# Five load buffers in place of three for the FFN's weights and the first FFN's modulation

## The chip, the cores and the metric

The kernel runs on one core of a Trainium2 chip. The metric is the device time of one execution in microseconds (us); lower is better. The kernel before took 2551.44 us, the median of three runs (2548.18 to 2554.93).

## What is computed

Two layers of a decoder on 256 tokens of width 2048 in float32. A conditioning vector c gives each layer six rows of 2048 numbers, the modulation. Each layer mixes tokens and then applies a SwiGLU FFN of width 5632, each behind an RMS norm that is scaled and shifted by the modulation, and each added to x through a gate from the modulation.

```python
c_act = silu(c)
for l in range(2):
    mod = c_act @ w_mod[l] + b_mod[l]                      # 2048 x 12288 weights
    shift1, scale1, gate1, shift2, scale2, gate2 = split(mod, 6)
    h = rms_norm(x, norm1_gain[l]) * (1 + scale1) + shift1
    x = x + gate1 * hybrid_token_mixer(h, ...)             # w_in, three mixers, w_out
    h = rms_norm(x, norm2_gain[l]) * (1 + scale2) + shift2
    x = x + gate2 * ((silu(h @ w_gate[l]) * (h @ w_up[l])) @ w_down[l])
return rms_norm(x, final_norm_gain)
```

All weights are read from device memory in each execution, about 600 MB with everything.

## The kernel before

**A job.** The large products run as a stream of jobs. A job is one 128 x 1024 block of weights, 512 KB. `load` brings it into a tile `raw` (line 321, issued on SP's queue). ACT rounds it into a tile `wh` (line 328), DVE takes the rest, `wl = raw - wh` (line 329), and `products` multiplies it on TensorE (PE, line 356): three terms (high by high, high by low, low by high), two column halves and two blocks of 128 tokens make 12 matmuls of 512 columns. An FFN has 264 such jobs: columns of w_gate and w_up in pairs of 512-column chunks, and the rows of w_down in two groups, after chunks 0 to 5 and 6 to 10. At the end of a pair of chunks DVE multiplies silu(gate) by up (line 1136, tile `s`), PE transposes it (line 401) and ACT and DVE split it into the left operands for w_down.

**The modulation.** It runs in the background: after each job `tick` adds a rate and, when the sum passes one, takes the next step of `mod_segment`. A step loads 512 KB of w_mod into a tile `mraw` (line 218, SP's queue too) and multiplies and adds it on DVE (line 221, SCALAR_TENSOR_TENSOR, below STT). In the first FFN the rate is 0.4 steps a job (0.6 in its first pair of chunks), in the second 0.25. The first step of an FFN waits for the norm: POOL copies one number of the norm's last high part `hm` into the `mraw` tile ahead of its load (line 216, `hold`). Finished segments are summed over partitions with a few small PE instructions (`fin`).

**Buffers.** Tiles come from pools, and a tile of a tag goes round the pool's buffers:

```python
    rawp = ctx.enter_context(tc.tile_pool(name="rawp", bufs=3))
    modp = ctx.enter_context(tc.tile_pool(name="modp", bufs=3))
    wsp = ctx.enter_context(tc.tile_pool(name="wsp", bufs=3))
```

So the load of job n waits until `wl` of job n-3 has been computed from the same buffer. `wh` and `wl` have three buffers each, and ACT's split of job n waits for PE's matmuls of job n-3. Each FFN opens a pool of its own, `ffn_0` and `ffn_1`, in memory that the mixers have left.

**The order.** The program is written in order of dataflow, and a scheduler then sets the order of each engine's instructions; the engines and SP's queue keep to it. The FFN begins while the output projection ends: the norm ahead of the FFN (lines 439 to 449: scale on DVE, transpose on PE, scale and shift on ACT, tile `s`, and a split into `hm` on ACT and DVE) runs for the two token blocks, and PE fills the gaps with the FFN's first jobs. In the second FFN a load of the final gain, tile `fg`, 1 MB, also stands on SP's queue there (line 1126).

Of the kernel before, what the change touches and what calls it, by code (L numbers as in the profile page):

```python
# [19 lines left out]
P = 128  # L20
# [4 lines left out]
DEPTH = 2  # L25
# [78 lines left out]
def trunk(ctx: ExitStack, tc, x, cT, pos, small, consts, b_mod, w_mod, w_in, w_gk, w_out,  # L104
# [4 lines left out]
    rawp = ctx.enter_context(tc.tile_pool(name="rawp", bufs=3))  # L109
    modp = ctx.enter_context(tc.tile_pool(name="modp", bufs=3))  # L110
# [16 lines left out]
    def tl(pool, shape, tag, dt=F32, bufs=None):  # L127
        return pool.tile(shape, dt, tag=tag, name=nm(tag), bufs=bufs)
# [18 lines left out]
        return ap.to_broadcast(shape)  # L147


    ct = tl(kp, [P, N_FULL], "consts")  # L150
    SY.dma_start(ct, consts[:, :N_FULL])
    n_mask = CONSTS.shape[1] - N_FULL
# [27 lines left out]
    for name, turn in (("sin", 0.0), ("cos", 0.25)):  # L180
        n = tl(kp, [P, NB, 8], "turns" + name)
# [17 lines left out]
    def mod_segment(l, part, k0, nk):  # L199

        width = nk * P
        early = l == 0 and part in (SHIFT1, SCALE1)
        rows = (512 if early else 1024) // width
        st = {}

        def step(i):
            c0 = part * D + k0 * P
            if i == 0:
                st["acc"] = scr[1]() if early else tl(accp, [P, 1024], "acc")
                G.memset(st["acc"][:, :width], 0.0)  # L210
                SY.dma_start(st["acc"][0:1, :width], b_mod[l:l + 1, c0:c0 + width])
            acc = st["acc"][:, :width]
            n = min(rows, KD - i)
            raw = scr[1]() if early else tl(modp, [P, 1024], "mraw")
            if hold:
                G.tensor_copy(raw[:, 0:1], hold.pop())
            raw = raw[:, :n * width].rearrange("p (a n) -> p a n", a=n)
            SY.dma_start(raw, w_mod[l, i * P:(i + n) * P, c0:c0 + width]
                         .rearrange("(a p) n -> p a n", p=P))
            for a in range(n):  # L220
                V.scalar_tensor_tensor(acc, raw[:, a], c_act[:, i + a:i + a + 1], acc,  # L221
                                       ALU.mult, ALU.add)
            if i + n == KD:
                fins.append([FIN_LAG, lambda: finish(acc)])

        def finish(acc):
            if part in (GATE1, GATE2):
                g = tl(gatep, [P, 1024], "gate")
                for j in range(width // 512):
                    src = acc[:, j * 512:(j + 1) * 512]  # L230
                    t = tl(modp, [P, 2, 512], "mraw", F32R)
                    A.activation(t[:, 0], src, AF.Copy)
                    V.tensor_tensor(t[:, 1], src, t[:, 0].bitcast(F32), ALU.subtract)
                    ps = tl(psf, [P, 512], "fin")
                    for i in range(2):
                        TE.matmul(ps, ones_r, t[:, i], start=i == 0, stop=i == 1)  # L236
                    A.activation(g[:, j * 512:(j + 1) * 512], ps, AF.Copy)
                    gate_row[l, part, k0 // 4 + j] = g[:, j * 512:(j + 1) * 512]
                return
            t = tl(smp, [P, nk], f"mod{part}_{k0}_{nk}")  # L240
            sums = tl(smp, [P, nk], f"sums{nk}")
            for j in range(0, nk, 4):
                ps = tl(psf, [P, 512], "fin")
                n = min(4, nk - j)
                for i in range(n):
                    TE.transpose(ps[:, i * P:(i + 1) * P],  # L246
                                 acc[:, (j + i) * P:(j + i + 1) * P], ident)
                V.tensor_reduce(sums[:, j:j + n],
                                ps[:, :n * P].rearrange("p (a b) -> p a b", a=n), AX.X, ALU.add)
            if part in (SHIFT1, SHIFT2):  # L250
                V.tensor_copy(t, sums)
            else:
                o = (0 if part == SCALE1 else KD) + k0
                V.scalar_tensor_tensor(t, sums, 1.0, gains[:, l, o:o + nk],  # L254
                                       ALU.add, ALU.mult)
            for j in range(nk):
                mod_col[l, part, k0 + j] = t[:, j:j + 1]

        return [((l, part), lambda i=i: step(i)) for i in range(0, KD, rows)]


# [29 lines left out]
    def stream(groups, ks, lhs, whole=(), lead=(), tail=()):  # L291
# [19 lines left out]
        def load(job, n, place):  # L311
            segs, _, offs, runs, _, _, k = job
            width = sum(s[2] for s in segs)
            if k in whole:
                which[1] += 1
                pool, tag = ((rawp, "raw"), (wsp, "wh"), (wsp, "wl"))[which[1] % 3]
                raw = tl(pool, [P, 1024], tag)
            else:
                raw = tl(rawp, [P, 1024], "raw")
            for w, c, m, o in runs:  # L320
                SY.dma_start(raw[:, o:o + m], w[k * P:(k + 1) * P, c:c + m])
            cuts = [(raw[:, o:o + s[2]], s[2]) for s, o in zip(segs, offs)]
            if k in whole:
                return [(r, None) for r, _ in cuts]
            if place is None:
                wh = tl(wsp, [P, 1024], "wh", F32R)
                wl = tl(wsp, [P, 1024], "wl", F32R)
                A.activation(wh[:, :width], raw[:, :width], AF.Copy)  # L328
                V.tensor_tensor(wl[:, :width], raw[:, :width], wh[:, :width].bitcast(F32),  # L329
                                ALU.subtract)  # L330
                return [(wh[:, o:o + s[2]], wl[:, o:o + s[2]]) for s, o in zip(segs, offs)]
            res = []
            for r, m in cuts:
                wh, wl = place()[:, :m], place()[:, :m]
                A.activation(wh, r, AF.Copy)
                V.tensor_tensor(wl, r, wh.bitcast(F32), ALU.subtract)  # L336
                res.append((wh, wl))
            return res
# [36 lines left out]
    def ahead(wsp_n, hm_n):  # L375
        return (None,) * wsp_n + (at_hm,) * hm_n
# [79 lines left out]
    scr = [None, None]  # L456
# [490 lines left out]
    def layer(l):  # L947
        wi, wo = w_in[l], w_out[l]
        load_small(l)
        blocks, at = [], 0  # L950
# [91 lines left out]
        for bi, ks in enumerate(blocks):  # L1042
# [8 lines left out]
            if l == 0 and first:  # L1051
                for o in range(0, n_mask, 512):
                    n = min(512, n_mask - o)
# [64 lines left out]
        with ExitStack() as st:  # L1118
            pl = st.enter_context(tc.tile_pool(name=f"ffn_{l}", bufs=1, reuse_waits="tile"))
            scr[0] = lambda: tl(pl, [P, 512], "s", bufs=8)  # L1120

            closed.discard((l, GATE2))
            if l == DEPTH - 1:
# [26 lines left out]
            for chunks in (range(0, 6), range(6, 11)):  # L1150
# [15 lines left out]
                for half in range(2):  # L1166
                    gemm([(wd, half * 1024, 512), (wd, half * 1024 + 512, 512)],
                         [c * 4 + i for c in chunks for i in range(4)], lhs_a,
                         lambda blk, j, ps, half=half, final=final: add_gated(
                             l, GATE2, blk, half * 2 + j, ps, final),  # L1170
                         tail=ahead(*TAIL_FFN) if half and final else ())

    for l in range(DEPTH):
        layer(l)
# [41 lines left out]
```

## Time and profile before

| | |
|---|---|
| median of three runs | 2551.44 us (2548.18 to 2554.93) |
| the profiled execution | 2549.07 us |
| its span, first to last instruction | 2547.1 us |
| first FFN | about 547 to 1326 us of the span |
| second FFN | about 1785 to 2530 us |
| mean granted TensorE clock | 0.99 |
| read from device memory | 597 MB, 235 GB/s over the span |

The page gives the busy time of each engine. A row of instructions reads: line, engine, operation, tile written <- tiles read, shape, count, busy time, mean duration, and in brackets or behind a bar the idle time before it and what ended it. PEld is TensorE's loading of weights, which overlaps its matmuls. A row of windows gives for a stretch of the span the busy time of PE, PEld, DVE, ACT and POOL (with instruction counts), the granted TensorE clock as a share of full speed, the busy share of the DMA engines and GB/s. A row of waits gives who waited for whom, us in total, times, and the longest. SPq rows are DMA issues on SP's queue; their length is the issue's, not the transfer's. For several merged issues (x3) it runs from the first to the last.

### The profile page before, as it was taken

To read this page: it belongs to the slowest core of one execution; us is meant where nothing else is said; L and a number is where in the kernel's file an instruction comes from. 1 tells how busy PE (TensorE), PEld (TensorE's weight loads), DVE (VectorE), ACT (ScalarE), POOL (GpSimd) and SP (SyncE) were. 2 spreads that over 40 slices of the span, in tenths; PEclk is the share of its full clock that TensorE was granted. 3 is DMA by queue.
4 is the path that set the end of the run, shared out by engine and by line. 5 is a ranking of instruction groups with operands and counts; after the bars stand their busy time and mean duration, and the time that the engine had idled before them with its cause. 6 is when DMAs were issued, how large, how long until landed. Compare 5 with 4: busy or idle time off the path is not lost. (4 is left out here: it accounts for less than half of the span.)

```text
span 2547.1 us, 30770 instructions
## 1 busy us (share of the span) xinstructions
PE 2422.7 (95%) x11164; PEld 1881.8 (74%) x11164; DVE 1715.0 (67%) x2171; ACT 1052.3 (41%) x1546; POOL 57.3 (2%) x117
## 2 busy tenths in 40 slices
PE   4999999999999999999989999989999999999998
PEld 2555886458778777888768778867777888888876
DVE  7767977667777677657677775897666455554554
ACT  2103444044444333444344554555534443344443
POOL 1000000000000000000000000000000000000000
PEclk9999999999999999999999999999999999999999
DMA  9996568849888778778778841765778655666654
GB/s 345 374 335 209 181 193 274 291 172 316 280 274 304 262 263 281 267 219 286 233 245 284 287 117 55 257 221 174 253 258 272 189 187 187 190 187 194 187 178 157
DMA packets 190031, 600.76 MB, mean 236 GB/s; under 512 B 21628, under 2 KB 26268, under 8 KB 189496
## 3 DMA queue, kind: packets, MB, share of 16 engines
q1 hardware_dynamic: 189880, 598.81, 71.2%
q8 instruction: 87, 1.43, 0.2%
q14 instruction: 64, 0.52, 0.1%
HBM read 596.63 MB, written 2.10 MB: 235 GB/s over the span
## 5 line engine op out<-in xcount | busy, mean ns | idle before, releaser
L356 PE MATMUL acc<-wh,hm 128*128 128x512 f32 (+3 forms) x4872 | 1333.4, 388 | 17.3 <-ACT acc L414 5.1
L328 ACT ACTIVATE wh<-raw 128x1024 fp32r<-128x1024 f32 (+3 forms) x669 | 685.1, 1026 | 1012.2 <-PE acc L356 575.5
L329 DVE TENSOR_TENSOR wl<-raw,wh 128x1024 fp32r<-128x1024 f32 (+3 forms) x669 | 785.7, 1179 | 464.2 <-ACT wh L328 461.0
L356 PEld LDWEIGHTS acc<-wh,hm 128*128 128x128 f32 x4872 | 890.7, 189 | 212.4 <-issue 20.3
L356 PE MATMUL acc<-wl,hm 128*128 128x512 f32 (+3 forms) x2484 | 793.3, 394 | 6.2 <-DVE wl L329 4.8
L356 PEld LDWEIGHTS acc<-wl,hm 128*128 128x128 f32 x2484 | 458.3, 189 | 116.2 <-issue 18.7
L221 DVE SCALAR_TENSOR_TENSOR acc<-mraw,c_act,acc 128x1024 f32<-128x1024 f32 x320 | 410.1, 1282 | 156.8 <-DMA mraw<-in_w_mod 154.1
L356 PE MATMUL acc<-wh,ahl 128*128 128x512 f32 x560 | 157.8, 396 | 0.0
L356 PEld LDWEIGHTS acc<-wh,ahl 128*128 128x128 f32 x560 | 105.6, 189 | 24.5
L221 DVE SCALAR_TENSOR_TENSOR g<-g,c_act,g 128x512 f32<-128x512 f32 x128 | 88.7, 746 | 11.5 <-DMA g<-in_w_mod 11.5
L356 PE MATMUL acc<-wl,ahl 128*128 128x512 f32 x280 | 90.7, 397 | 3.0 <-DVE wl L329 3.0
L356 PE MATMUL acc<-wh,b 128*128 128x512 f32 (+2 forms) x184 | 72.8, 535 | 2.2 <-ACT b L445 2.1
L356 PE MATMUL acc<-raw,b 128*128 128x512 f32 (+2 forms) x176 | 66.6, 517 | 0.0
L356 PE MATMUL acc<-wl,b 128*128 128x512 f32 (+2 forms) x176 | 66.1, 512 | 0.2 <-DVE g L967 0.2
L356 PEld LDWEIGHTS acc<-wl,ahl 128*128 128x128 f32 x280 | 52.6, 189 | 17.2 <-DVE wl L329 5.2
L356 PEld LDWEIGHTS acc<-wh,b 128*128 128x128 f32 x184 | 34.8, 194 | 31.7 <-issue 23.6
L927 DVE TENSOR_TENSOR acc<-acc,gate 128x512 f32<-128x512 f32 x64 | 42.8, 692 | 20.0 <-PE acc L356 20.0
L445 ACT ACTIVATE b<-mm,mod,mod 128x128 f32<-128x128 f32 x24 | 9.2, 458 | 108.9 <-DVE mod L254 91.3
L356 PEld LDWEIGHTS acc<-wl,b 128*128 128x128 f32 x176 | 32.6, 190 | 26.7 <-issue 21.5
L356 PEld LDWEIGHTS acc<-raw,b 128*128 128x128 f32 x176 | 32.7, 190 | 26.1 <-issue 21.8
L210 POOL MEMSET acc<- 128x1024 f32 x20 | 19.0, 954 | 1019.4 <-PE fin L246 709.7
L929 DVE TENSOR_TENSOR xs<-xs,acc 128x512 f32<-128x512 f32 x64 | 41.6, 678 | 0.1
(312 smaller groups left out, 1639.7 us busy)
## 6 DMA issues: line engine op xcount, KB each, us to landing
mraw<-in_w_mod SPq DMA_DIRECT2D x320, 512.0 KB
raw<-in_w_down SPq DMA_DIRECT2D x176, 512.0 KB
raw<-in_w_gate SPq DMA_DIRECT2D x160, 512.0 KB
raw<-in_w_up SPq DMA_DIRECT2D x160, 512.0 KB
raw<-in_w_in SPq DMA_DIRECT2D x72, 512.0 KB
g<-in_w_mod SPq DMA_DIRECT2D x128, 256.0 KB
raw<-in_w_out SPq DMA_DIRECT2D x43, 512.0 KB
raw<-in_w_in SPq DMA_DIRECT2D x32, 264.0 KB
```

The source lines that it names most:

```text
L210: G.memset(st["acc"][:, :width], 0.0)
L221: V.scalar_tensor_tensor(acc, raw[:, a], c_act[:, i + a:i + a + 1], acc, ALU.mult, ALU.add)
L328: A.activation(wh[:, :width], raw[:, :width], AF.Copy)
L329: V.tensor_tensor(wl[:, :width], raw[:, :width], wh[:, :width].bitcast(F32), ALU.subtract)
L356: TE.matmul(ps[blk, j][:, :segs[j][2]], xa, parts[j][part], start=i == 0 and n == 0, stop=last and n == len(terms) - 1)
L445: A.activation(h32[:, i], ps[:, i * P:(i + 1) * P], AF.Identity, scale=mod_col[l, 3 * sub + 1, at + i], bias=mod_col[l, 3 * sub, at + i])
L927: V.tensor_tensor(ps, ps, need(gate_row, (l, part, j)), ALU.mult)
L929: V.tensor_tensor(x_j, x_j, ps, ALU.add)
```

## The change

During an FFN the `raw` tiles take turns over five buffers, three of the pool `rawp` and two with the tag `raw2` in the FFN's own pool. In the first FFN the `mraw` tiles do the same, with `mraw2`. The turn is counted in the program's order, it goes on from where the stage before left it, and the counts are cleared at the end of each FFN. In the `finish` of a gate the tile `mraw` still comes from the three. All line numbers below the new function move by 9 (321 is now 330, 218 is 227).

```diff
+    room, turns = {}, {}
+
+    def in_turn(pool, tag, n):
+        more, m = room.get(tag, (None, 0))
+        at = turns[tag] = (turns.get(tag, -1) + 1) % (n + m)
+        return tl(pool, [P, 1024], tag) if at < n else tl(more, [P, 1024], tag + "2", bufs=m)
...
-            raw = scr[1]() if early else tl(modp, [P, 1024], "mraw")
+            raw = scr[1]() if early else in_turn(modp, "mraw", 3)
...
-                raw = tl(rawp, [P, 1024], "raw")
+                raw = in_turn(rawp, "raw", 3)
...
         with ExitStack() as st:
             pl = st.enter_context(tc.tile_pool(name=f"ffn_{l}", bufs=1, reuse_waits="tile"))
             scr[0] = lambda: tl(pl, [P, 512], "s", bufs=8)
+            room["raw"] = pl, 2
+            if l < DEPTH - 1:
+                room["mraw"] = pl, 2
...
+            room.clear()
+            turns.clear()
```

The scheduler gives another order. Three places follow, as rows of one engine: line, operation, tile written <- tensor or tile read, shape. The number that ends a tile's name tells the job: in the first FFN 4021 is job 0, 4043 job 1, 4068 job 2, 4086 job 3, 4107 job 4, 4128 job 5; in the second 14080, 14102, 14120, 14138, 14156, 14174.

SP's queue at the start of the first FFN, before:

```order
L321 DMA raw_1031_4021<-in_w_gate 128x1024
L211 DMA acc_1041_4061<-in_b_mod 1x1024
L321 DMA raw_1038_4043<-in_w_gate 128x1024
L321 DMA raw_1043_4068<-in_w_gate 128x1024
L211 DMA acc_1181_4763<-in_b_mod 1x1024
L321 DMA raw_1046_4086<-in_w_gate 128x1024
L321 DMA raw_1050_4107<-in_w_gate 128x1024
L321 DMA raw_1054_4128<-in_w_gate 128x1024
L218 DMA mraw_1049_4104<-in_w_mod 128x1024
L218 DMA mraw_1042_4064<-in_w_mod 128x1024
```

and now:

```order
L330 DMA raw_1031_4021<-in_w_gate 128x1024
L220 DMA acc_1041_4061<-in_b_mod 1x1024
L227 DMA mraw_1053_4125<-in_w_mod 128x1024
L227 DMA mraw_1060_4164<-in_w_mod 128x1024
L330 DMA raw_1046_4086<-in_w_gate 128x1024
L227 DMA mraw_1067_4203<-in_w_mod 128x1024
L220 DMA acc_1181_4763<-in_b_mod 1x1024
L330 DMA raw_1050_4107<-in_w_gate 128x1024
L330 DMA raw_1054_4128<-in_w_gate 128x1024
L330 DMA raw2_1038_4043<-in_w_gate 128x1024
L227 DMA mraw2_1042_4064<-in_w_mod 128x1024
L330 DMA raw2_1043_4068<-in_w_gate 128x1024
```

Jobs 1 and 2 have the added buffers and their loads now stand behind those of jobs 3 to 5, and job 2's behind a load into `mraw2`, which is the one that POOL's copy holds for the norm (the tile numbered 4064, as before). On ACT the same place reads now

```order
L457 ACTIVATE hm_1022_3985<-s_1021_3984 128x512
L454 ACTIVATE s_1026_4000<-mm_1030_4005,mod3_8_8_949_3713,mod4_8_8_998_3894 128x128 x3
L457 ACTIVATE hm_1027_4001<-s_1026_4000 128x512
L337 ACTIVATE wh_1039_4045<-raw2_1038_4043 128x1024
L337 ACTIVATE wh_1044_4070<-raw2_1043_4068 128x1024
L337 ACTIVATE wh_1047_4088<-raw_1046_4086 128x1024
```

where `hm_1027_4001` is the norm's last high part. Before, `wh` of jobs 1 and 2 stood ahead of the norm's first `s`, and `wh` of job 3 just ahead of that last `hm`.

SP's queue at the start of the second FFN, before:

```order
L321 DMA raw_3128_14080<-in_w_gate 128x1024
L321 DMA raw_3135_14102<-in_w_gate 128x1024
L321 DMA raw_3138_14120<-in_w_gate 128x1024
L321 DMA raw_3141_14138<-in_w_gate 128x1024
L321 DMA raw_3144_14156<-in_w_gate 128x1024
L321 DMA raw_3147_14174<-in_w_gate 128x1024
L218 DMA mraw_3214_14535<-in_w_mod 128x1024
L1126 DMA fg_3127_14078<-in_final_gain 128x2048
```

and now:

```order
L330 DMA raw_3128_14080<-in_w_gate 128x1024
L330 DMA raw_3141_14138<-in_w_gate 128x1024
L330 DMA raw_3144_14156<-in_w_gate 128x1024
L330 DMA raw_3147_14174<-in_w_gate 128x1024
L227 DMA mraw_3214_14535<-in_w_mod 128x1024
L1138 DMA fg_3127_14078<-in_final_gain 128x2048
L330 DMA raw2_3135_14102<-in_w_gate 128x1024
L330 DMA raw2_3138_14120<-in_w_gate 128x1024
L227 DMA mraw_3201_14459<-in_w_mod 128x1024
```

Jobs 1 and 2 moved behind `fg`. That load now waits for the DVE half of the norm's last `hm` and for the norm's last transposes on PE; before, it issued after those transposes. On ACT `wh` of jobs 1 and 2 moved behind the norm's last `hm` here too.

Inside the FFNs the load of job n now waits for `wl` of job n-5. The `mraw` loads and their multiply-adds (on DVE) keep their order among themselves and move against the jobs. One of them, `mraw_1211_4916` near the end of the first pair of chunks, shows how. SP's queue before:

```order
L321 DMA raw_1175_4727<-in_w_gate 128x1024
L218 DMA mraw_1204_4877<-in_w_mod 128x1024
L321 DMA raw_1178_4745<-in_w_gate 128x1024
L321 DMA raw_1188_4784<-in_w_gate 128x1024
L218 DMA mraw_1211_4916<-in_w_mod 128x1024
L321 DMA raw_1191_4802<-in_w_gate 128x1024
```

and DVE's rows around its multiply-add before (a `wl` tile's second number is its `raw` tile's plus 3):

```order
L329 TENSOR_TENSOR wl_1180_4748<-raw_1178_4745,wh_1179_4747 128x1024
L329 TENSOR_TENSOR wl_1190_4787<-raw_1188_4784,wh_1189_4786 128x1024
L221 SCALAR_TENSOR_TENSOR acc_1181_4763<-mraw_1211_4916,c_act_8_100,acc_1181_4763 128x1024
L329 TENSOR_TENSOR wl_1193_4805<-raw_1191_4802,wh_1192_4804 128x1024
L329 TENSOR_TENSOR wl_1197_4826<-raw_1195_4823,wh_1196_4825 128x1024
```

Now SP:

```order
L330 DMA raw_1145_4605<-in_w_up 128x1024
L227 DMA mraw2_1228_5012<-in_w_mod 128x1024
L330 DMA raw_1149_4626<-in_w_up 128x1024
L330 DMA raw2_1152_4644<-in_w_up 128x1024
L227 DMA mraw_1211_4916<-in_w_mod 128x1024
L330 DMA raw2_1168_4705<-in_w_gate 128x1024
```

and DVE:

```order
L230 SCALAR_TENSOR_TENSOR acc_1181_4763<-mraw_1204_4877,c_act_8_100,acc_1181_4763 128x1024
L338 TENSOR_TENSOR wl_1137_4551<-raw2_1135_4548,wh_1136_4550 128x1024
L338 TENSOR_TENSOR wl_1141_4572<-raw2_1139_4569,wh_1140_4571 128x1024
L338 TENSOR_TENSOR wl_1144_4590<-raw_1142_4587,wh_1143_4589 128x1024
L230 SCALAR_TENSOR_TENSOR acc_1181_4763<-mraw_1211_4916,c_act_8_100,acc_1181_4763 128x1024
L230 SCALAR_TENSOR_TENSOR acc_1181_4763<-mraw2_1221_4973,c_act_8_100,acc_1181_4763 128x1024
```

Before, the load followed the raw load of 4784, and the multiply-add followed `wl` of that same job. Now the load follows the raw load of 4644 and the multiply-add `wl` of 4587, three jobs apart (4587, 4605, 4626, 4644). The load comes four jobs earlier in the stream than before, the multiply-add seven.

## The prediction

> **What bounds the kernel now.** I read the page's busy shares and the chain that ended last first, then compared the two FFN stages by windows, then listed the waits inside the first of them, and last the order of time where each FFN starts.
>
> ```profile
> span 2547.1 us, 30770 instructions
> PE 2422.7 (95%) x11164; PEld 1881.8 (74%) x11164; DVE 1715.0 (67%) x2171; ACT 1052.3 (41%) x1546; POOL 57.3 (2%) x117
> PE 24%; DMA 4%; DVE 2%; issue 1%; ACT 1%; POOL 0%; SPq 0%; ACTq 0%; POOLq 0%; DVEq 0%
> ```
>
> TensorE (PE) is busy for 95% of the span, so no change that only moves loads can bring more than the idle PE time of the stages that it touches. It touches the two FFNs. The next rows are windows from the start of each FFN's job 3 (below) to its last matmul. A job is one 512 KB block of weights and the 12 matmuls of 512 columns on it.
>
> ```profile
> core 0: us, PE busy (x) PEld busy (x) DVE busy (x) ACT busy (x) POOL busy (x), PEclk, DMA share, GB/s
> 562.70:1325.00 762.30, 743.48 (x3265) 604.26 (x3266) 528.89 (x490) 312.23 (x334) 7.02 (x8) 0.99 0.80 271
> 1794.50:2529.50 735.00, 726.77 (x3202) 593.87 (x3203) 407.52 (x380) 309.35 (x331) 0.72 (x1) 1.00 0.66 207
> ...
> 1976.14 50.37 PE acc L356 x222
> ```
>
> The same 261 jobs take 762.3 us in the first FFN and 735.0 in the second. PE idles 18.8 us in the first (762.30 - 743.48) and 8.2 in the second (735.00 - 726.77). The last row, from the chain in order of time, gives the pace when nothing is late: 50.37 / 222 = 0.227 us for a matmul, 2.72 for a job. In the first FFN DVE works harder (529 us against 408), because more of the modulation (the `mraw` loads and the multiply-adds on line 221) runs there. What is late there, by the waits of that stage:
>
> ```profile
> ACT wh L328 <- PE acc L356: 173.7, 114, 6.0
> DVE acc L221 <- DMA mraw<-in_w_mod: 81.4, 69, 3.8
> ACT wh L328 <- DMA raw<-in_w_up: 75.9, 42, 3.6
> ACT wh L328 <- DMA raw<-in_w_down: 59.9, 30, 3.8
> ACT wh L328 <- DMA raw<-in_w_gate: 49.3, 29, 4.6
> ACT wh L328 <- DVE acc L221: 36.7, 19, 5.3
> PE acc L356 <- DVE wl L329: 5.2, 9, 1.2
> PE mm L401 <- DVE s L1136: 4.9, 2, 3.3
> ```
>
> ACT waits for raw weights in 101 jobs, 185 us; in the other jobs it waits for PE, so the splits are already ahead. PE itself feels little of this: 5.2 us of waits for `wl`, 4.9 for the product `s` at a chunk's end. The rest of PE's loss comes after such stalls, as stretches at half the granted clock:
>
> ```profile
> 740.40:743.81 3.41, 3.41 (x11) 2.62 (x10) 2.85 (x6) 1.65 (x2) 0.00 (x0) 0.50 0.78 258
> 836.00:839.41 3.41, 3.41 (x14) 2.91 (x14) 2.90 (x4) 2.16 (x4) 0.00 (x0) 0.51 0.96 330
> 1262.60:1266.00 3.40, 3.40 (x10) 2.63 (x9) 3.40 (x5) 1.04 (x4) 0.00 (x0) 0.50 0.95 359
> 1307.00:1310.40 3.40, 3.40 (x9) 2.50 (x9) 2.06 (x4) 2.11 (x4) 0.00 (x0) 0.50 0.54 170
> 1877.00:1883.83 6.83, 5.97 (x18) 4.85 (x19) 5.29 (x9) 2.25 (x3) 0.00 (x0) 0.50 0.65 202
> ```
>
> Each half-clock stretch of 3.41 us costs 1.7: 6.8 in the first FFN, 3.4 in the second.
>
> **The change, part by part.** Nothing is removed or added in work: the same loads, splits and matmuls. Two things move.
>
> *Inside the FFNs (a gain).* The load of job n now waits for `wl` of job n-5, not n-3, so it lands before ACT wants it, and the ACT waits above mostly go. What that is worth is bounded by PE's losses, not ACT's: from below by the waits booked to `wl`, 5.2 us, from above by all idle and half-clock time of the stage, 18.8 + 6.8 = 25.6. The second FFN, where ACT already waits for PE in most jobs, still loses 8.2 + 3.4 = 11.6, so I take 25.6 - 11.6 = 14. The five `mraw` buffers I value at nothing beyond that. In the order shown with the change, a `mraw` load follows the raw load three jobs ahead of the split that its multiply-add follows, where it followed that same job's or the next one's. But the raw load three ahead waits for `wl` two jobs back, as the next one's did before, so the `mraw` load leaves no sooner, and DVE's 81.4 us of waits for `mraw` stay about as they are. Their cover is DVE's slack, 762 - 529 = 233 us; without it a late STT would delay the `wl` behind it. In the second FFN only raw gains: its ceiling is 11.6, and I take 3 (0 to 7), since its one large stall stands behind a `mraw` wait.
>
> *At the start of each FFN (a loss).* Before, jobs 0, 1 and 2 were loaded and split ahead of the norm that precedes the FFN, and their 36 matmuls ran between the norm's transposes:
>
> ```profile
> 546.50:562.69 16.19, 9.26 (x36) 6.43 (x37) 1.00 0.28 97
> ...
> 526.97 1.06 ACT L328 ACTIVATE wh<-raw 128x1024 fp32r<-128x1024 f32 x1 [52.56 <-DMA raw<-in_w_gate]
> 533.05 1.06 ACT L328 ACTIVATE wh<-raw 128x1024 fp32r<-128x1024 f32 x1
> 541.73 1.06 ACT L328 ACTIVATE wh<-raw 128x1024 fp32r<-128x1024 f32 x1 [0.70 <-PE acc L356]
> 561.50 1.14 ACT L328 ACTIVATE wh<-raw 128x1024 fp32r<-128x1024 f32 x1
> 562.45 0.71 ACT L448 ACTIVATE hm<-s 128x512 fp32r<-128x512 f32 x1
> 562.69 1.20 PE L356 MATMUL acc<-wh,hm 128*128 128x512 f32 x4 [0.99 <-ACT wh L328]
> ```
>
> Now jobs 1 and 2 take the two added buffers, and the order puts their loads and splits behind. Only job 0's 12 matmuls fill the norm. In the first FFN job 1's split follows the last `hm`, which a missing split (about 0.95) lets end at 562.2; job 1 then starts about 563.2, when job 3 started before. Job 2 is worse: its load stands on SP behind an added `mraw` load that waits for POOL's copy of the norm's last `hm`. For both, the second FFN has the durations:
>
> ```profile
> 1791.54 0.33 SPq L1126 DMA_DIRECT2D fg<-in_final_gain  x1
> 1794.53 1.20 PE L356 MATMUL acc<-wh,hm 128*128 128x512 f32 x4 [0.38 <-ACT wh L328]
> 1795.06 0.72 POOL L216 COPY mraw<-hm 128x1 f32<-128x1 f32 x1 [11.62 <-ACT hm L448]
> 1795.65 0.69 DVE L449 TENSOR_TENSOR hm<-s,hm 128x512 fp32r<-128x512 f32 x1
> 1795.76 3.20 SPq L321 DMA_DIRECT2D raw<-in_w_gate  x3
> 1799.53 1.06 ACT L328 ACTIVATE wh<-raw 128x1024 fp32r<-128x1024 f32 x1 [2.64 <-DMA raw<-in_w_gate]
> ...
> 1792.50:1793.50 1.00, 1.00 (x6) 0.82 (x5) 0.69 (x1) 1.00 (x4) 0.00 (x0) 1.00 1.09 352
> 1793.50:1794.50 1.00, 0.65 (x3) 0.19 (x2) 0.00 (x0) 1.00 (x3) 0.00 (x0) 1.00 0.97 410
> ```
>
> From issue to use a load takes 1799.53 - 1795.76 = 3.77 us, and 512 KB at 352 to 410 GB/s take 1.3 to 1.5 of it. Job 2 of the first FFN: `hm` 562.2, copy 0.72, the `mraw` issue 0.4, so its load goes out at 563.4 and lands at 567.1, or 568.5 if it shares with the `mraw`; with the split it starts at 568.2 to 569.6 and job 3 at 570.9 to 572.3. Against 562.69 that is 8.2 to 9.6; I take 9. Second FFN: the load of `fg` (the final gain, 1 MB) now waits for the norm's last DVE `hm` and stands ahead of jobs 1 and 2. That `hm` ended at 1796.3 and moves to between 1792.7 and 1794.7, with a split and a `wl` out of its way and 24 matmuls fewer among the transposes. Job 1's load goes out 0.35 later, lands 3.77 later plus 2.6 to 3.0 for `fg`'s megabyte, and is split in 1.1: start 1800.5 to 1802.9. Before, job 3 started at 1794.53, so job 1's equivalent was two jobs earlier, 1789.1. Loss 11.4 to 13.8; I take 12.5. PE idles before each late job, so a half-clock stretch may follow: 0 to 1.7 at the first start, 0 to 3.4 at the second, 1.7 taken together.
>
> [...]
>
> Sum: 9 + 12.5 + 1.7 = 23 lost at the starts (18 to 29 with both ends), 14 + 3 = 17 gained inside (5 to 33). Net +6. The profiled execution took 2549.07 us (span 2547.1 and about 2 around it), so 2555; the median of the runs is 2.4 above that execution, so 2557.
>
> **The rivals.**
> - *Slower, over 0.3%: PE was covered inside anyway.* PE waited for `wl` 5.2 us in the whole first FFN; ACT's 185 us of lateness were taken up by the splits ahead. If 5 us inside is all, and the `mraw` chain keeps the stalls at chunk ends, the time is 2551 + 23 - 5 = 2569. It decides when less than about 15 us of the 25.6 come back. For it: the small row of `wl`. Against it: the half-clock stretches and the 27 us by which the first FFN is longer.
> - *Faster, over 0.3%: the starts cost less than the order says.* SP, ACT and DVE run ahead of one another on the chip, and what follows a late start finds five buffers full and the modulation ahead. With half the start loss (12) and 20 + 3 inside: 2551 - 11 = 2540. For it: DVE has 233 us of slack. Against it: `fg` and the copy are true waits, ahead of the loads on one in-order queue.
> - *No change at all.* PE-bound at 95%: the start is regained by the next chunk's end and the interior gives as little: 2551.
>
> **How the numbers follow.** A measurement here tells 0.3%, 7.7 us, from no change. Forecast (both effects near their sizes, net -1 to +14) 0.52, of it 0.36 within and 0.16 slower; the slower rival 0.22; the faster one 0.16; no change 0.10, of it 0.06 within and 0.02 on each side. So faster 0.18, same 0.42, slower 0.40. The forecast's own range is 2550 to 2565; with the rivals' middle parts it reaches 2541 to 2572.
>
> **What would show it.** ACT's waits for `raw` in the first FFN fall from 185 us to under 60, and DVE's for `mraw` stay near 80. Job 1's first matmul comes after the norm's last `hm`, with a PE idle of 1 to 4 us around job 2 in the first FFN and 5 to 9 us ahead of job 1 in the second, ended by ACT `wh`, behind DMA raw2. From the end of job 2 to the last matmul the first FFN falls from 762 to about 748 and the second from 735 to 732. I am wrong if jobs 1 and 2 run inside the norm, if PE's idle in the first FFN does not fall, or if the `mraw` waits vanish.

## The result: slower by 0.5%

| | before | changed |
|---|---|---|
| median | 2548.18 us (7 runs, 2546.09 to 2554.93) | 2563.93 us (7 runs, 2557.48 to 2568.65) |
| ratio to before | | 1.0051, 95% interval 1.0033 to 1.0068 |
| span of the profiled execution | 2547.1 us | 2566.0 us |

The change made the kernel 15.75 us slower in the median. The forecast was +6, inside "no change", with 2541 to 2572 as the range. Sign and range held; the size did not. The change is more than the 0.3% that the prediction called no change, so the outcome fell into "slower", which it gave 0.40, where "same" had 0.42.

**Where the time went.** PE does the same 9012 weight matmuls (the line that was 356) in both kernels. Counting them from the first, and taking the time between the same counts in each trace, cuts the executions into stages. The limits are the starts of matmuls 1140, 1252, 4300, 5800 and 5900, which lie before at 546.5, 582.1, 1323.1, 1765.0 and 1799.6 us of the span. Around the two starts the order differs a little between kernels, so the limits lie a few jobs to each side.

| stage | before, us | changed |
|---|---|---|
| up to the first FFN's start | 506.6 | +4.8 |
| first FFN's start | 35.6 | +10.8 |
| first FFN, the rest | 741.0 | -8.9 |
| between the FFNs | 441.9 | +0.3 |
| second FFN's start | 34.5 | +14.6 |
| second FFN, the rest | 735.9 | -2.5 |

The starts lose 25.4 us and the insides gain 11.4, which is +14.0 for what the change touches. The 4.8 ahead of it lie where both programs are alike, and come back below. The first start's stage runs past the place at which the prediction's window for the inside begins (job 3's first matmul, 562.69); the section on the prediction uses that place.

**The changed kernel's waits in the first FFN** (us in total, times, longest), to be held against those shown of before:

```profile
ACT wh L337 <- PE acc L365: 388.0, 233, 5.3
DVE acc L230 <- DMA mraw<-in_w_mod: 81.1, 51, 4.6
ACT wh L337 <- DMA raw<-in_w_gate: 10.2, 4, 4.9
PE acc L365 <- DVE wl L338: 7.4, 9, 2.2
```

ACT waited for raw loads 185 us before; now it waits for PE nearly always, so the loads do arrive earlier. DVE's waits for the modulation's loads are what they were, 81 us. And PE still waits for `wl`.

**The start of the first FFN**, ACT, POOL, SP and PE in order of time:

```profile
569.06 0.63 ACT L457 ACTIVATE hm<-s 128x512 fp32r<-128x512 f32 x1
569.59 1.04 ACT L337 ACTIVATE wh<-raw 128x1024 fp32r<-128x1024 f32 x1
569.75 0.71 POOL L225 COPY mraw<-hm 128x1 f32<-128x1 f32 x1 [11.43 <-ACT hm L457]
570.48 0.33 SPq L227 DMA_DIRECT2D mraw<-in_w_mod  x1
570.86 0.43 SPq L330 DMA_DIRECT2D raw<-in_w_gate  x1
575.55 2.01 ACT L337 ACTIVATE wh<-raw 128x1024 fp32r<-128x1024 f32 x2 [4.91 <-DMA raw<-in_w_gate]
...
570.69 0.98 PE L365 MATMUL acc<-wh,hm 128*128 128x512 f32 x2 [3.72 <-ACT wh L337]
576.66 0.73 PE L365 MATMUL acc<-wh,hm 128*128 128x512 f32 x2 [1.01 <-ACT wh L337]
```

Job 1's split follows the norm's last `hm`, and PE's first matmul on it comes at 570.69. Job 2's load goes out at 570.86, after POOL's copy and the held modulation load, and is split 4.7 us later. The norm itself has a longer hole too: with fewer matmuls to fill it PE stands 5.42 us where it stood 2.33, and what follows up to 567 us runs at half the clock.

```profile
558.98 1.94 PE L451 MATMUL mm<-consts,s 128*128 128x128 f32 x8 [5.42 <-DVE s L448]
...
553.00:570.70 17.70, 7.15 (x26) 5.15 (x24) 7.65 (x16) 13.46 (x33) 1.27 (x2) 0.71 0.15 56
558.98:567.00 8.02, 6.58 (x22) 4.98 (x22) 2.43 (x5) 5.56 (x14) 0.00 (x0) 0.50 0.00 0
```

**The start of the second FFN:**

```profile
1800.06 0.63 ACT L457 ACTIVATE hm<-s 128x512 fp32r<-128x512 f32 x1
1801.49 0.33 SPq L1138 DMA_DIRECT2D fg<-in_final_gain  x1
1801.87 0.90 SPq L330 DMA_DIRECT2D raw<-in_w_gate  x2
1807.46 1.06 ACT L337 ACTIVATE wh<-raw 128x1024 fp32r<-128x1024 f32 x1 [6.77 <-DMA raw<-in_w_gate]
1808.57 1.22 PE L365 MATMUL acc<-wh,hm 128*128 128x512 f32 x2 [10.60 <-ACT wh L337]
...
1808.50:1812.50 4.00, 3.89 (x8) 2.65 (x9) 3.75 (x4) 2.02 (x3) 0.00 (x0) 0.50 0.95 335
```

SP stands at `fg` until the norm ends; job 1's load follows it and is usable 1807.46 - 1801.87 = 5.6 us later; PE idles 10.60 us and then runs job 1 at half its clock (0.50 from 1789.5, inside the norm, to 1813.1 us). The kernel reached this place 7.0 us later than before (+4.8, +10.8, -8.9, +0.3), so job 1's equivalent in the kernel before (1789.1) moves to 1796.1, and 12.5 us are lost up to the first matmul, the rest with the half clock (the 4.5 us from 1808.57 at 0.50).

### The profile page after: what moved, and what is told of

Same layout as the page of the kernel before. It is cut to its first block, busy times and chain, and to the rows that moved or that the text cites. A ratio compares the mean times of both kernels' runs of the same rounds, so it can differ in the third digit from the quotient of the medians.

```text
span 2566.0 us, 30742 instructions
## 1 busy us (share of the span) xinstructions
PE 2429.8 (95%) x11164; PEld 1892.0 (74%) x11164; DVE 1712.0 (67%) x2171; ACT 1054.7 (41%) x1546; POOL 56.5 (2%) x117
## 5 line engine op out<-in xcount | busy, mean ns | idle before, releaser
L230 DVE SCALAR_TENSOR_TENSOR g<-g,c_act,g 128x512 f32<-128x512 f32 x128 | 88.6, 748 | 11.6 <-DMA g<-in_w_mod 11.5
L365 PEld LDWEIGHTS acc<-wl,ahl 128*128 128x128 f32 x280 | 52.6, 188 | 14.6 <-DVE wl L338 2.5
L365 PEld LDWEIGHTS acc<-wh,b 128*128 128x128 f32 x184 | 35.1, 195 | 31.6 <-issue 23.5
```

Of the source, the lines that this page charges most:

```text
L365: TE.matmul(ps[blk, j][:, :segs[j][2]], xa, parts[j][part], start=i == 0 and n == 0, stop=last and n == len(terms) - 1)
```

## The experiments

Theory A: the loss is the place of jobs 1 and 2, behind the norm, and the inside of the FFNs gains. Rival B: the loss is inside, from more loads in flight. Each run's ratio is to runs of the kernel before on the same chip, and is given as recorded; it is not the quotient of the two medians. The stage differences of all runs stand in one table at the end of this section.

### The added buffers come in at the seventh load

```diff
+        if skip.get(tag, 0):
+            skip[tag] -= 1
+            return tl(pool, [P, 1024], tag)
         at = turns[tag] = (turns.get(tag, -1) + 1) % (n + m)
...
             room["raw"] = pl, 2
+            turns["raw"], skip["raw"] = 2, 6
             if l < DEPTH - 1:
                 room["mraw"] = pl, 2
+                turns["mraw"], skip["mraw"] = 2, 3
```

> The change with one edit: in each FFN the first six raw loads (and the first three modulation loads of the first FFN) go round the old three buffers, and the added ones come in from the seventh (fourth) on, so jobs 1 and 2 stand ahead of the norm again. Theory A (the loss is the place of jobs 1 and 2 at the two FFN starts, about 10 + 14 us, and the inside of the FFNs gains about 9 + 2): 2535 to 2542 us, job 3 of each FFN starts where it did before (562.7 and 1794.5 from the span's start, plus what earlier stages shift). Rival B (the loss comes from more loads in flight and an earlier modulation inside the FFNs): 2555 to 2565, the starts make no difference.

Measured: 2539.88 us (12 runs), before 2549.18; ratio 0.9978 (0.9960 to 0.9996). Both start losses are gone (-0.8 and -1.5 us against before) and the inside keeps its gain (-10.8 and -2.3). Job 3 of the second FFN starts behind the norm with a short idle, as before:

```profile
1779.72 1.20 PE L368 MATMUL acc<-wh,hm 128*128 128x512 f32 x4 [0.96 <-ACT wh L340]
```

Theory A holds. The same buffers, taken up five raw loads later (the seventh in place of the second), make the kernel faster than before, though by little: the interval ends at 0.9996.

### The raw weights alone, the modulation alone

For the raw weights alone:

```diff
             room["raw"] = pl, 2
-            if l < DEPTH - 1:
-                room["mraw"] = pl, 2
```

> The change for the raw weights alone; the modulation keeps three buffers. Theory A: both starts are lost as in the change, and the inside gains as much or a little less: 2560 to 2567 us. If the modulation's earlier place on DVE causes the stalls of the first 180 us of the first FFN (about 7 us in the changed profile), 2555 to 2559. Rival B: about half of the change's loss, 2553 to 2558.

Measured: 2571.67 us (6 runs), before 2549.18; ratio 1.0098 (1.0073 to 1.0123). The modulation alone:

```diff
-            room["raw"] = pl, 2
             if l < DEPTH - 1:
                 room["mraw"] = pl, 2
```

> The change for the modulation alone; raw weights keep three buffers. Theory A: jobs 1 and 2 stand ahead of the norm as before, so no start is lost, and ACT still waits for raw loads: 2545 to 2551 us, no change. Rival B: slower, 2553 to 2560, with the stalls of the first 180 us.

Measured: 2549.74 us (12 runs); ratio 1.0011 (0.9991 to 1.0032). The raw buffers carry the whole loss, and the modulation's buffers do nothing that can be measured. Raw alone was 5 us above the top of what I expected; its profiled execution has 8.2 us more between the FFNs, a stage that the change does not touch, so this excess may be no sign of what the modulation's buffers are worth. A later run (six on the old buffers, raw alone) looks at that again.

### The added raw buffers come in at the fourth load

```diff
-            turns["raw"], skip["raw"] = 2, 6
+            turns["raw"], skip["raw"] = 2, 3
```

> As the run with six, but the added raw buffers come in from the fourth load on: jobs 0 to 2 run inside the norm, jobs 3 and 4 are loaded behind the held modulation load and behind the final gain. Theory A: the loss moves to job 3 and shrinks, about 6 us in the first FFN (start near 569 in place of 562.7) and 8 in the second (near 1803 in place of 1794.5), less the gain inside: 2548 to 2554 us. Rival B: as the change, 2560 to 2567.

Measured: 2547.68 us (10 runs), at the lower edge of what was expected; ratio 1.0005 (0.9984 to 1.0026). Now jobs 0 to 2 run inside the norm and job 3 is late: +7.7 us at the first start and +5.0 at the second, where PE waits

```profile
1795.57 1.22 PE L368 MATMUL acc<-wh,hm 128*128 128x512 f32 x2 [4.80 <-ACT wh L340]
```

and the insides give back 9.5 and 5.0. The loss moves with the job that has the added buffer, as A says; of its two sizes the first was 7.7 where 6 was expected, the second 5.0 where 8 was.

### The change, with nothing held on SP's queue

```diff
-                SY.dma_start(fg[0], final_gain.to_broadcast([P, D]))
...
             for chunks in (range(0, 6), range(6, 11)):
+                if chunks[0] and l == DEPTH - 1:
+                    SY.dma_start(fg[0], final_gain.to_broadcast([P, D]))
...
-                hold[:] = [res[3][1][:, 0, 0:1].bitcast(F32)]
+                hold[:] = [res[3][1][:, 0, 0:1].bitcast(F32)] if l else []
```

> The change with its buffers where it has them, but nothing held on SP's queue ahead of jobs 1 and 2: the final gain's load is issued in the middle of the second FFN, and the first FFN's first modulation load doesn't wait for the norm. Their raw loads are then issued before the norm ends; only their splits still stand behind it on ACT. Theory A splits each start's loss: two jobs that no longer fill the norm (5.4 us), and the late load behind it (3 to 4 in the first FFN, 7 in the second). It expects the second part to go: PE's idle before job 1 of the second FFN falls from 10.6 us to 2 to 4, and the time to 2549 to 2556 us. If the splits' place behind the norm is all that counts: 2560 to 2566.

Measured: 2553.88 us (12 runs), before 2551.13; ratio 1.0019 (0.9999 to 1.0038). At the second FFN's start SP issues both loads 22 us ahead of the norm's end, and the loss falls from 14.6 to 6.2 us:

```profile
1777.28 0.91 SPq L330 DMA_DIRECT2D raw<-in_w_gate  x2
1799.31 0.63 ACT L457 ACTIVATE hm<-s 128x512 fp32r<-128x512 f32 x1
1799.85 1.04 ACT L337 ACTIVATE wh<-raw 128x1024 fp32r<-128x1024 f32 x1
1800.94 1.10 PE L365 MATMUL acc<-wh,hm 128*128 128x512 f32 x2 [4.39 <-ACT wh L337]
```

What is left is ACT's order: the split of job 1 stands behind the norm, and PE has two jobs (5.4 us) fewer to fill it with. At the first start, where the load was held less long (in the changed kernel SP stands there from 552.6 to 570.5 us, at the second start from 1777.0 to 1801.5), the loss falls only from 10.8 to 8.8. So the second start's 14.6 us are about 8 of queue and 6 of order; the first start's are mostly order and the half clock in the norm (0.50 from 558.98 to 567.00 us in the changed kernel; in this run the hole is 5.41 us, and the eight transposes behind it take 1.94 us as there).

### Six loads on the old buffers, raw weights alone

```diff
             room["raw"] = pl, 2
             turns["raw"], skip["raw"] = 2, 6
-            if l < DEPTH - 1:
-                room["mraw"] = pl, 2
-                turns["mraw"], skip["mraw"] = 2, 3
```

> The run with six loads on the old buffers, for the raw weights alone; the modulation keeps three. If the gain inside comes from raw loads that land earlier: 2538 to 2544 us, as with both. If the modulation's own buffers bring half of it, as the difference between the change and the change for raw alone suggests (7.7 us): 2545 to 2550.

Measured: 2535.9 us (7 runs), before 2551.13; ratio 0.9929 (0.9902 to 0.9956). No worse than with the modulation's buffers: these bring nothing that can be told. The two comparisons point opposite ways, each beyond its intervals: leaving these buffers out made the change slower (1.0098 against 1.0051) and this version faster (0.9929 against 0.9978). The runs of the second pair were on different chips, and what that alone does to such a ratio was not measured, so I read neither difference of half a per cent as an effect. This is a version that beats both kernels, by 15 us in the medians against before.

### Four buffers, and six

Four in all, of each kind:

```diff
-            room["raw"] = pl, 2
+            room["raw"] = pl, 1
-                room["mraw"] = pl, 2
+                room["mraw"] = pl, 1
```

> The run with six loads on the old buffers, with one added buffer each (four in all) in place of two. The raw load then waits for the split four jobs back. If the fourth buffer covers a load's 3.8 us and the split's 2.3: as with five, 2538 to 2544 us. If each buffer counts alike, half of the gain: 2543 to 2548.

Measured: 2541.1 us (12 runs); ratio 0.9958 (0.9938 to 0.9977). Six raw buffers:

```diff
-            room["raw"] = pl, 2
+            room["raw"] = pl, 3
```

> The run with six loads on the old buffers, with three added raw buffers (six in all), five for the modulation. With five, ACT no longer waits for raw loads, so a sixth has nothing to bring: 2536 to 2543 us. If what is left of PE's stalls is bursts of late loads: 2530 to 2536.

Measured: 2536.54 us (10 runs); ratio 0.9936 (0.9913 to 0.9960). Four buffers of each kind lie between the two runs with five raw ones (0.9978 and 0.9929), and so does the sixth: these runs don't tell four, five and six apart.

### What is left inside: multiply-adds that don't wait

In the changed kernel the longest stall inside the first FFN looks like this on DVE and PE:

```profile
759.31 1.28 DVE L230 SCALAR_TENSOR_TENSOR acc<-mraw,c_act,acc 128x1024 f32<-128x1024 f32 x1 [4.57 <-DMA mraw<-in_w_mod]
760.51 0.68 DVE L1148 TENSOR_TENSOR s<-s,acc 128x512 f32<-128x512 f32 x1
...
761.25 1.12 PE L410 MATMUL ga<-consts,s 128*128 128x128 f32 x4 [4.57 <-DVE s L1148]
```

DVE stands at a multiply-add whose load is late, the product `s` is behind it in order, and PE waits 4.57 us for `s`. The next two kernels take that wait away and keep the loads and the amount of DVE's work; the multiply-adds read a `wl` tile, so the modulation of that stage is not computed:

```diff
+                if dry:
+                    dry[1:] = [wl]
...
-                V.scalar_tensor_tensor(acc, raw[:, a], c_act[:, i + a:i + a + 1], acc,
+                V.scalar_tensor_tensor(acc, dry[-1][:, :width].bitcast(F32) if len(dry) > 1 else raw[:, a],
+                                       c_act[:, i + a:i + a + 1], acc,
...
+            dry[:] = [1] if l == 0 else []
```

with five raw buffers from the seventh load on:

> The run with six loads on the old buffers for the raw weights alone, and in the first FFN the modulation's multiply-adds read the job's wl tile in place of the loaded columns: the same loads and the same DVE work, but DVE never waits for a modulation load. The modulation of that stage is thereby not computed. If what is left of PE's stalls in the first FFN comes from DVE standing at a multiply-add with a late load, ahead of wl and of the product s: 6 to 10 us less than without this edit, 2526 to 2531 us. If the stalls have another cause: 2533 to 2538.

and with the three of the kernel before:

> The kernel before with the same edit (three raw buffers, multiply-adds of the first FFN that don't wait for their loads; the modulation of that stage is not computed). If late raw loads stall PE by themselves: 2543 to 2549 us, little gained. If PE was stalled only where DVE stood at a late modulation load, and more raw buffers merely let it catch up after: 2532 to 2539, about as much gained as with the added raw buffers.

Measured: 2526.5 us (6 runs; ratio 0.9906, 0.9888 to 0.9924) and 2529.25 us (8 runs; ratio 0.9937, 0.9912 to 0.9962). The waits from 575 to 1310 us, first with five raw buffers and the wait, then with five and without, then with three and without:

```profile
DVE acc L233 <- DMA mraw<-in_w_mod: 94.2, 63, 3.8
PE acc L368 <- DVE wl L341: 4.6, 8, 1.3
PE mm L413 <- DVE s L1150: 4.0, 1, 4.0
```

```profile
ACT wh L343 <- PE acc L371: 366.4, 224, 5.3
DVE acc L234 <- DMA mraw<-in_w_mod: 13.3, 8, 3.1
```

```profile
ACT wh L331 <- PE acc L359: 248.4, 153, 5.7
ACT wh L331 <- DMA raw<-in_w_down: 69.1, 38, 4.2
ACT wh L331 <- DMA raw<-in_w_up: 36.7, 22, 3.2
ACT wh L331 <- DMA raw<-in_w_gate: 30.8, 18, 3.2
DVE acc L222 <- DMA mraw<-in_w_mod: 8.8, 7, 2.1
```

The rest of the first FFN took 741.0 us before. Without the waits for the modulation it takes 13.1 less with three raw buffers and 23.5 less with five; with the waits, five buffers bring 8.2 (raw alone). So there are two causes: the modulation's multiply-adds cost 13 to 15 us here, and the raw loads' short lead 8 to 10. PE's own waits say the same: those for `s` and `wl` in this stage sum to 11.9 us before, 11.2 in the changed kernel and 11.8 with five raw buffers from the seventh load on, raw alone, but to 2.5 and 2.3 in the two kernels without waits. My two alternatives for the second kernel were too far apart. It gained as much as "only the modulation" asks for, and a little more, but ACT still waits 137 us for raw loads in it, and the added buffers still bring 10.4 there.

Three things limit these sizes. Each is one execution, and the two without waits were the fastest of their six and eight; all runs with five or six raw buffers that keep the waits and SP's queue lie between -6.2 and -10.8. The medians of the two kernels without waits are only 2.8 us apart and their intervals overlap, so that the two gains add is argued from the stage, not shown by the times. And the edit does more than remove waits: 32 of the stage's 122 multiply-adds, in its last third, keep their loads. The others stand more evenly on DVE, 34 of all in the first thousand weight matmuls of the stage where 50 and 49 stood. SP is held less at modulation loads (25 us in place of 45, with three raw buffers). How much of the 13 to 15 us is the late load and how much is the place of the multiply-add was not told apart. Both kernels also ran the second FFN 5.4 and 8.1 us faster, where the edit is not in force; that stays open, and their whole times overstate what the edit does to the first FFN.

### The modulation's loads on a queue of their own

```diff
-            SY.dma_start(raw, w_mod[l, i * P:(i + n) * P, c0:c0 + width]
+            (SY if early or not apart else G).dma_start(raw, w_mod[l, i * P:(i + n) * P, c0:c0 + width]
...
+            apart[:] = [1] if l == 0 else []
```

> The run with six loads on the old buffers (both raw and modulation with five), and in the first FFN the modulation's loads are issued on POOL's queue in place of SP's, so each waits only for its own buffer and not behind raw loads that are held. If SP's order is why the added modulation buffers bring nothing: DVE's waits for the modulation in the first FFN fall from about 81 us to under 30 and the time to 2525 to 2533 us. If POOL's issue is slower than what it saves, or the loads crowd the raw loads: 2538 to 2550.

> As the run with POOL's queue, with three modulation buffers and five raw ones. If the added modulation buffers count once their loads aren't held on SP: 4 us or more slower than with five, DVE's waits for the modulation 40 us or more. If three are enough with the queue of their own: the same time as with five.

Measured: 2574.97 us (6 runs; ratio 1.0109, 1.0080 to 1.0137) with five modulation buffers and 2569.03 us (6 runs; ratio 1.0091, 1.0066 to 1.0116) with three. The expectation fell. DVE's waits for the modulation don't fall (70.4 us in 50 waits on SP's queue, in the run with six loads on the old buffers and both kinds with five), and PE waits longer for `wl` (4.8 us there); the first run's rows, the last from the DMA issues with KB each and the median us from issue to landing:

```profile
DVE acc L234 <- DMA mraw<-in_w_mod: 80.7, 32, 7.5
PE acc L369 <- DVE wl L342: 18.2, 13, 3.0
...
mraw<-in_w_mod POOLq DMA_DIRECT2D x96, 512.0 KB, 6.9
```

In the first run the waits are fewer but longer (32 of up to 7.5 us in place of 50 of up to 3.5). In the second they hardly change: 71 of up to 3.3 us, 97.8 in total, where the run with raw alone on SP's queue has 63 of up to 3.8, 94.2 in total; yet PE waits 21.5 us for `wl` there and the stage is 25.6 us longer. So longer waits are not the whole account.

Nor is a slow queue shown. A load issued by POOL needs 6.9 us to land (median; 6.1 in the second run). Taking modulation loads and multiply-adds in order, those multiply-adds that waited for their load ran 6.0 us (median of 62) after SP had issued it in the run with raw alone, and 6.0 (median of 67, 59 of them POOL's) in the second run here: the same. What the edit also changed is DVE's order. In this stage two multiply-adds stand back to back 23 and 18 times, where the two runs on SP's queue have 12 and 7, and 37 and 32 of them stand in its first 500 weight matmuls, where those have 25 and 23. Most of PE's stalls in the second run follow two late multiply-adds with at most one `wl` between them, but no run kept that order and changed the queue alone, so which of them costs the time stays open. That SP's order is why the added modulation buffers bring nothing is thereby not shown; it stays an argument from the order.

### All runs by stage

Differences to the profiled execution of before, us, one execution each; the times differ by some us from run to run without any change (2546.09 to 2554.93 us in the seven runs of before).

| run | up to FFN 1 | start 1 | rest of FFN 1 | between | start 2 | rest of FFN 2 |
|---|---|---|---|---|---|---|
| the change | +4.8 | +10.8 | -8.9 | +0.3 | +14.6 | -2.5 |
| from the seventh load | -5.1 | -0.8 | -10.8 | +2.9 | -1.5 | -2.3 |
| raw alone | +0.1 | +10.6 | -6.6 | +8.2 | +15.5 | -1.2 |
| modulation alone | -4.8 | -1.2 | +1.6 | +1.8 | 0.0 | -2.7 |
| from the fourth load | -3.5 | +7.7 | -9.5 | +3.5 | +5.0 | -5.0 |
| nothing held on SP | +2.3 | +8.8 | -6.2 | +2.3 | +6.2 | -2.7 |
| seventh, raw alone | -3.3 | +0.5 | -8.2 | +2.6 | -1.5 | -0.3 |
| seventh, four buffers | -1.8 | -0.8 | -5.3 | +0.4 | -1.2 | +2.0 |
| seventh, six raw | -0.3 | -0.9 | -7.1 | +1.8 | -1.3 | -1.0 |
| seventh, raw, no waits | -3.1 | -0.7 | -23.5 | +3.2 | -1.1 | -5.4 |
| before, no waits | -3.1 | +0.5 | -13.1 | +1.1 | -1.1 | -8.1 |
| POOL's queue, five | -4.4 | +6.7 | +19.4 | +4.2 | -1.7 | -7.4 |
| POOL's queue, three | -5.3 | +4.6 | +17.4 | +6.7 | -1.4 | -3.7 |

The start columns part cleanly: all runs that give jobs 1 and 2 the added buffers have +8.8 to +10.8 and +6.2 to +15.5, those with no added raw buffer up to job 5 and SP's queue as it was have -1.5 to +0.5.

## Why the prediction was right in kind and low in size

The prediction's window for the inside begins at job 3's first matmul. Counted to there, the first start lost 13.0 us and the second 15.1, and from there to the end the insides gained 11.0 and 3.0. These are the figures to hold against its terms.

**The starts (23 us predicted, 28.1 measured): the mechanism right, the first start priced too low.** The mechanism was read from the order of SP and ACT and priced from the rows of before, and each step shows in the trace: job 1's split behind the last `hm`, job 2's load behind the copy and the held load, jobs 1 and 2 of the second FFN behind `fg`. The second start was priced at 12.5 up to the first matmul, and 12.5 were lost; the rest is for the most part job 1 at half the clock (4.5 us at 0.50), as allowed for. The first start was priced at 9 and lost 13.0. The prediction let the norm's last `hm` end at 562.2. It ended at 569.69, or 565.0 without the 4.7 us by which the kernel reached this stage later, so 2.8 after the forecast: the norm itself is slower in the changed kernel (a hole of 5.42 us in place of 2.33, then half the clock). Job 1 then ran at 0.55 of the clock from 570.69 to 574.50. Job 2's late load, to which the prediction gave 2.3 to 3.7 us, made PE wait only 1.01 us for the split. The 10.8 of the stage table look closer to 9 by chance: the kernel before takes 2.2 us longer than the changed one from job 3 to the end of that stage.

The 1.7 us for half clock at both starts was an estimate from the stretches of 3.41 and 6.83 us. Job 1 alone ran 3.81 us at 0.55 at the first start and 4.5 us at 0.50 at the second, which cost about 1.7 and 2.2 us. At the second start PE's 10.60 us of idle stand ahead of it, but the clock was at 0.50 from 1789.5 us on, when PE still had matmuls of the norm to do, so the trace doesn't show that this idle brought the half clock. The low end of the starts' sum was added wrongly: 8.2 + 11.4 is 19.6, not 18.

**The inside of the first FFN (14 us predicted, 11.0 measured): the step whose reasoning failed.** The window that took 762.30 us before took 751.27:

```profile
580.33:1331.60 751.27, 738.11 (x3266) 602.82 (x3265) 521.29 (x486) 311.70 (x332) 6.29 (x7) 0.99 0.80 271
```

The 14 read: the idle and half-clock time of the stage, 25.6 us, less what the second FFN still loses, 11.6. That took the whole difference between the two FFNs as the raw loads' doing. The runs without waits show that 13 to 15 us belong to the modulation's multiply-adds, which the change leaves alone: I had said that the waits for `mraw` would stay, and the trace agrees (81.4 and 81.1 us), but I let DVE's 233 us of slack cover them. Slack over a stage is no cover where DVE runs in order and `s` or `wl` stands behind the late multiply-add (DVE's 4.57 us at 759.31 became PE's 4.57 us at 761.25). So PE's waits for these two stayed, from 582.1 us to the end of the first FFN's stage and at the same jobs of the changed kernel:

```profile
PE acc L356 <- DVE wl L329: 5.0, 8, 1.2
PE mm L401 <- DVE s L1136: 4.9, 2, 3.3
PE ga L401 <- DVE s L1136: 2.0, 1, 2.0
```

```profile
PE acc L365 <- DVE wl L338: 6.6, 7, 2.2
PE ga L410 <- DVE s L1148: 4.6, 1, 4.6
```

What the five raw buffers took away are PE's other waits, 6.2 us in this stage down to 1.6, and some half-clock time: four stretches of 3.4 us before, 13.6 us in all, and now one of 3.4 and one of 6.8 us (625.60:629.02 and 758.72:765.55 at 0.50), 10.2 in all. Counted from job 3, the runs with five or six raw buffers that keep the waits and SP's queue gain 7.7 to 11.6 us; the term should have been about that.

**The modulation's buffers (nothing predicted): right.** Alone they change nothing that can be measured (1.0011), and without them the version from the seventh load is no slower.

**The inside of the second FFN (3 predicted, 3.0 measured): right in size, from one execution.** The other runs with added raw buffers have -7.4 to +2.0 there, and the two in which that FFN is as before have -2.7 and -8.1, so the hit may be luck.

**The sum.** 28.1 - 14.0 is +14.1 us, where the prediction had +6: 5 of the 8 missing are the starts, the first above all, and 3 are the insides. The absolute forecast, 2557, missed by only 7 because the kernel before came out at 2548.18 in place of 2551.44. The rival "slower, PE was covered inside" was nearer: it gave +18. Its own condition, less than about 15 us of the 25.6 come back, was met, and so was its reason that the `mraw` chain keeps the stalls at chunk ends; only its 5 us inside were too few. So part of the hit is the width of the range. The rival "the starts cost less than the order says" fell. Of the signs named in advance, ACT's waits for raw loads, DVE's for `mraw` and the place of job 1 came true; PE's idle ahead of job 1 in the second FFN was 10.60 us where 5 to 9 were named.

## What to carry to other kernels

When a ring of buffers grows, look at which job takes the first added one. The scheduler here placed the loads into them after work that the old buffers' loads had been ahead of, and the starts lost 25 us by it; the same raw buffers, taken up from the seventh load on, made the kernel 9 to 15 us faster than before in the medians.

DVE, which works in order here, had 230 us of slack over the changed kernel's stage (751.27 - 521.29), and PE still waited 4.57 us for an `s` that stood behind one late multiply-add. Price a wait by what stands behind it on its engine and by who waits for that, not by the engine's idle time over the stage.

A large wait on an engine that is off the path (ACT's 185 us) can vanish and return a twentieth of it (8.9 us).

## What the runs showed that I had not expected

**A stall of a microsecond can be followed by a slowdown that costs five.** The 4.8 us ahead of the first FFN arise for the most part at one place, where both programs are alike: the changed kernel comes there 1.9 us earlier than the kernel before and leaves it 3.3 us later. PE waits there for a load of w_out, before and then in the changed kernel:

```profile
401.49 1.12 PE L356 MATMUL acc<-wl,hm 128*128 128x512 f32 x2 [1.02 <-DMA wl<-in_w_out]
...
400.00:411.00 11.00, 9.98 (x38) 5.44 (x38) 3.51 (x5) 4.79 (x6) 0.00 (x0) 1.00 0.97 356
```

```profile
399.93 1.73 PE L365 MATMUL acc<-wl,hm 128*128 128x512 f32 x2 [1.38 <-DMA wl<-in_w_out]
...
399.90:411.00 11.10, 11.07 (x22) 5.62 (x23) 2.63 (x4) 4.20 (x5) 0.00 (x0) 0.54 0.82 316
```

With 1.02 us of wait the clock stays at 1.00; with 1.38 the next 11 us run at 0.54, and PE does 22 matmuls there in place of 38. The length alone doesn't decide: in the run with six raw buffers PE waited 1.40 us at this place and the clock stayed at 1.00. Of all profiled executions here, the three that lost both starts slow down at this place (waits of 1.24, 1.38 and 1.72 us; 0.56, 0.56 and 0.62 of the clock from 399 to 410 us) and no other does (1.00). The work up to there is the same in all, so whether that is chance or not stays open.

**Half-clock stretches of 3.4 us followed single waits of 1.94 to 3.27 us.** Ahead of the first four half-clock stretches that the prediction shows (740.40, 836.00, 1262.60 and 1307.00 us), PE's last single waits were 2.01, 3.27, 1.94 and 2.00 us, and in the 3.4 us before each it was busy for 1.41, 0.57, 1.46 and 1.38 us. The waits ended 0.5 to 1.4 us ahead of the stretches. What brings the half clock was not measured.
